# Moving each store of a log-softmax kernel into the middle of the next tile's exponentials

## Chip, cores, metric

One core of one Trainium2 chip. The time is that of one execution on the device, in microseconds (us). Every run told here was fast, with a granted clock of 1.0. A ratio between two kernels is the mean time of one kernel's fast runs over that of the other's fast runs of the same rounds, so it is not quite the ratio of the medians that are quoted beside it.

## The reference

```python
# x: float32, 16 x 512 x 50000
max_x = np.max(x, axis=-1, keepdims=True)
shifted = x - max_x
log_sum_exp = np.log(np.sum(np.exp(shifted), axis=-1, keepdims=True))
return (shifted - log_sum_exp).astype(np.float32)
```

1638.4 MB come in and as many go out.

## The kernel before

A tile is 32 rows of x, each cut over 4 partitions: 128 partitions of 12,500 numbers, 6.4 MB. There are 256 tiles and four buffers of that size. A buffer goes round like this: SP issues the load; VectorE (DVE) takes the maxima in four quarters; ScalarE (ACT) takes the four exponentials with their sums; the sums are joined; DVE subtracts in place; ACT issues the store; and SP, when that store has landed, issues the load of the tile four further on into the same buffer. The first and the last tile go in four parts.

```python
NBUF = 4
NS = 4
...
# SP: a load follows the store that frees its buffer
with sync.Fori(0, rounds - 1) as q:
    for i in range(NBUF):
        j = (i + 1) % NBUF
        take(sync, stored[j])
        load(j, src(q, i))
...
# DVE, one whole tile
take(vector, landed[j])
for c in range(NS):
    vector.tensor_reduce(out=negms[j][:, c : c + 1], in_=bufs[j][:, cols(c)],
                         op=ALU.max, axis=AX, negate=True).then_inc(...)
...
subtract(j, bufs[j])
...
# ACT, one whole tile
def store(j, dst, buf):
    subtracted.next(scalar.dma_start(out=dst, in_=buf)).then_inc(stored[j], 16)

def whole(j, dst):
    for c in range(NS):
        shifted.next(scalar.activation(out=dump, in_=bufs[j][:, cols(c)], func=ACT.Exp, ...)).then_inc(on_act.sem)
        on_act.next(scalar.nop())
    agreed.next(scalar.activation(out=scales[j], in_=negms[j], func=ACT.Exp, ...)).then_inc(rescaled.sem)
    log(j)
    store(j, dst, bufs[j])        # waits for DVE's subtraction of this tile
```

## Time and profile before

| | before |
|---|---|
| time, median of the first 3 runs | 7574.89 us (7571.26 to 7595.91) |
| span of its profile | 7612.1 us |
| busiest compute engine | DVE, 72% |
| DMA queues, share of 16 engines | 50.2% + 49.8% |

The costliest groups and the DMA issues of the page of before. A group's columns are count, busy time and mean ns of one, then the engine's idle time ahead of them and what ended most of it; an issue's are count, size and median us from issue to landing.

```profile
L274 ACT ACTIVATE dump<-buf,negm 128x3125 f32<-128x3125 f32 x1016 | 2914.3, 2868 | 3807.2 <-DVE negm L221 3710.5
L221 DVE TENSOR_REDUCE negm<-buf 128x1 f32<-128x3125 f32 x1016 | 3391.7, 3401 | 943.6 <-DVEq L47 943.6
...
buf<-in_x_dram SPq DMA_DIRECT2D x254, 6250.0 KB, 39.9
out_dram<-buf ACTq DMA_DIRECT2D x254, 6250.0 KB, 52.6
```

ACT's idle time is ended by DVE's maxima, and DVE's by landed loads.

### The profile page before, as it was taken

The numbers are of one execution on the slowest core, as the hardware profiler recorded it, in microseconds if no ns is written. First come the engines' busy times: TensorE is split into PE (matmuls) and PEld (weight loads), VectorE is DVE, ScalarE is ACT, GpSimd is POOL, SyncE is SP. The second block draws the span as 40 slices with busy tenths as digits, with TensorE's granted clock in tenths as the row PEclk, the third lists the DMA queues.
The fourth block names the chain that finished last, engine by engine and source line by source line (L and its number), as shares of the span: only waits on it lengthen the run. The fifth ranks groups of instructions, "written<-read, shape, count | busy, mean of one in ns | idle before, by whom it ended". The sixth has DMA issues, their size and how long they took to land. (4 is left out here: it accounts for less than half of the span.)

```text
span 7612.1 us, 14101 instructions
## 1 busy us (share of the span) xinstructions
PE 478.8 (6%) x2048; PEld 456.4 (6%) x2048; DVE 5445.7 (72%) x2842; ACT 3185.1 (42%) x2565; POOL 2.3 (0%) x10
## 2 busy tenths in 40 slices
PE   0000000000000000000000000000000000000000
PEld 0000000000000000000000000000000000000000
DVE  7777777777776777777767777777777777777777
ACT  4344444434444344443443444434434444344443
POOL 0000000000000000000000000000000000000000
DMA  9999999999999999999999999999999999999999
GB/s 423 434 433 433 434 434 434 433 433 434 434 433 432 432 432 431 431 432 428 429 429 429 426 427 429 431 430 432 432 431 431 433 433 433 434 433 431 432 433 393
DMA packets 75458, 3276.85 MB, mean 430 GB/s; under 512 B 8384, under 2 KB 8384, under 8 KB 8384
## 3 DMA queue, kind: packets, MB, share of 16 engines
q1 hardware_dynamic: 37728, 1638.42, 50.2%
q10 hardware_dynamic: 37728, 1638.42, 49.8%
q14 instruction: 2, 0.02, 0.0%
HBM read 1638.40 MB, written 1638.40 MB: 430 GB/s over the span
## 5 line engine op out<-in xcount | busy, mean ns | idle before, releaser
L274 ACT ACTIVATE dump<-buf,negm 128x3125 f32<-128x3125 f32 x1016 | 2914.3, 2868 | 3807.2 <-DVE negm L221 3710.5
L221 DVE TENSOR_REDUCE negm<-buf 128x1 f32<-128x3125 f32 x1016 | 3391.7, 3401 | 943.6 <-DVEq L47 943.6
L211 DVE TENSOR_SCALAR buf<-buf,negmax,logsum 128x12500 f32<-128x12500 f32 (+1 forms) x262 | 1739.7, 6640 | 553.9 <-ACT logsum L265 553.9
L324 PE MATMUL sums<-scaled,ones 128*128 128x1 f32 x2032 | 474.1, 355 | 7061.9 <-DVE scaled L232 7061.9
L324 PEld LDWEIGHTS sums<-scaled,ones 128*128 128x128 f32 x2032 | 452.4, 328 | 7083.6 <-DVE scaled L232 7083.6
L232 DVE TENSOR_TENSOR scaled<-scale,part 128x4 f32<-128x4 f32 x254 | 41.2, 162 | 575.4 <-ACT scale L282 575.4
L265 ACT ACTIVATE logsum<-sums 128x1 f32<-128x1 f32 x262 | 44.8, 171 | 552.3 <-PE sums L324 546.9
L274 ACT ACTIVATION_READ_ACCUMULATOR dump<-buf,negm 128x1 f32 x1016 | 189.4, 186 | 0.0
L282 ACT ACTIVATE scale<-negm,negmax 128x4 f32<-128x4 f32 x254 | 75.5, 297 | 23.5
L226 DVE TENSOR_REDUCE negp<-negm 128x1 f32<-128x4 f32 x254 | 39.9, 157 | 38.9 <-DVE negm L221 38.9
L206 DVE STREAM_TRANSPOSE negmax<-spread 128x32 f32<-128x32 f32 x262 | 55.5, 212 | 9.1
L190 DVE STREAM_TRANSPOSE allneg<-negp 128x32 f32<-128x32 f32 x262 | 55.4, 212 | 9.1
L193 DVE TENSOR_REDUCE rowneg<-allneg 128x8 f32<-128x32 f32 (+1 forms) x262 | 48.8, 186 | 9.1
L200 DVE COPY spread<-rowneg 128x32 f32<-128x32 f32 x262 | 47.5, 181 | 9.1
L293 ACT ACTIVATE dump<-buf,negmax 128x3125 f32<-128x3125 f32 x8 | 22.9, 2869 | 30.9 <-DVE negmax L206 30.9
L239 DVE TENSOR_REDUCE negp<-buf 128x1 f32<-128x3125 f32 x8 | 27.2, 3399 | 8.1 <-DVEq L47 8.1
L335 PE MATMUL sums<-sub_sum,ones 128*128 128x1 f32 x16 | 4.7, 363 | 59.0 <-ACT dump L293 59.0
L335 PEld LDWEIGHTS sums<-sub_sum,ones 128*128 128x128 f32 x16 | 4.0, 312 | 59.6 <-ACT dump L293 59.6
L308 ACT ACT_TABLE_LOAD x1 | 1.3, 1283 | 1.0 <-SPq L115 1.0
L293 ACT ACTIVATION_READ_ACCUMULATOR dump<-buf,negmax 128x1 f32 x8 | 1.5, 186 | 0.0
L144 POOL TENSOR_SCALAR_AFFINE_SELECT ones<-ones 128x128 f32<-128x128 f32 x2 | 0.9, 442 | 0.1
L148 POOL TENSOR_SCALAR_AFFINE_SELECT ones<-ones 128x128 f32<-128x128 f32 x2 | 0.9, 428 | 0.1
(5 smaller groups left out, 0.8 us busy)
## 6 DMA issues: line engine op xcount, KB each, us to landing
buf<-in_x_dram SPq DMA_DIRECT2D x254, 6250.0 KB, 39.9
out_dram<-buf ACTq DMA_DIRECT2D x254, 6250.0 KB, 52.6
buf<-in_x_dram SPq DMA_DIRECT2D x8, 1562.5 KB, 27.6
out_dram<-buf ACTq DMA_DIRECT2D x8, 1562.5 KB, 18.3
```

The source lines that it names most:

```text
L190: vector.transpose(out=allneg, in_=negp.to_broadcast([P, SQ]))
L193: vector.tensor_reduce(out=rowneg[:, : SQ // g], in_=allneg.rearrange("p (r g) -> p r g", g=g), op=op, axis=AX, negate=negate,)
L200: vector.tensor_copy(out=spread.rearrange("p (r g) -> p r g", g=g), in_=rowneg[:, : SQ // g, None].to_broadcast([P, SQ // g, g]),)
L206: vector.transpose(out=negmaxs[k], in_=spread)
L211: vector.tensor_scalar(out=buf, in0=buf, scalar1=negmaxs[k][:, 0:1], scalar2=logs[k], op0=ALU.add, op1=ALU.subtract,)
L221: vector.tensor_reduce(out=negms[j][:, c : c + 1], in_=bufs[j][:, cols(c)], op=ALU.max, axis=AX, negate=True,).then_inc(shifted.sem if c < ...
L226: vector.tensor_reduce(out=negp, in_=negms[j], op=ALU.min, axis=AX).then_inc(on_dve.sem)
L232: vector.tensor_mul(out=scaleds[j], in0=scales[j], in1=parts[j])
L265: scalar.activation(out=logs[k], in_=rowsums[k], func=ACT.Ln)
L274: scalar.activation(out=dump, in_=bufs[j][:, cols(c)], func=ACT.Exp, bias=negms[j][:, c : c + 1], scale=1.0, accum_out=parts[j][:, c : c + 1],
L282: scalar.activation(out=scales[j], in_=negms[j], func=ACT.Exp, bias=negmaxs[j][:, 0:1], scale=-1.0,)
L324: ins = tensor.matmul(rowsums[j], ones[G], scaleds[j][:, c : c + 1], start=c == 0, stop=c == NS - 1,)
```

## The change

Its intent is to keep ACT from standing still behind the subtraction and to issue the store of a tile two exponentials into the next one. In the loop's first lap there is no earlier tile, so the first whole tile is taken out ahead of it; after the last tile one store is left over.

```diff
+GATE = 2
...
-        def whole(j, dst):
+        def whole(j, dst=None):
             for c in range(NS):
+                if c == GATE and dst is not None:
+                    store((j - 1) % NBUF, dst, bufs[(j - 1) % NBUF])
                 shifted.next(
...
             log(j)
-            store(j, dst, bufs[j])
...
+        whole(1)
+        settle()
         dst = run(ot, 1, rounds)
         with scalar.Fori(0, rounds) as q:
             for i in range(NBUF):
-                whole((i + 1) % NBUF, dst(q, i))
+                whole((i + 2) % NBUF, dst(q, i))
             settle()
-        for t in tail:
-            whole(t % NBUF, ot[t])
+        for t in tail[1:]:
+            whole(t % NBUF, ot[t - 1])
+        store(t % NBUF, ot[t], bufs[t % NBUF])
```

## The prediction

> **What bounds the kernel now.** I read the page from the top: first the spans, then the row of slices, then the queues, then the waits, then the timeline of two tiles, and last the time from issue to landing of loads and stores in several windows. The page of the kernel before:
>
> ```profile
> span 7612.1 us, 14101 instructions
> ...
> PE 478.8 (6%) x2048; PEld 456.4 (6%) x2048; DVE 5445.7 (72%) x2842; ACT 3185.1 (42%) x2565; POOL 2.3 (0%) x10
> ...
> DMA  9999999999999999999999999999999999999999
> ...
> q1 hardware_dynamic: 37728, 1638.42, 50.2%
> q10 hardware_dynamic: 37728, 1638.42, 49.8%
> ...
> HBM read 1638.40 MB, written 1638.40 MB: 430 GB/s over the span
> ```
>
> No compute engine is busy for more than 72%, while the DMA row is 9 in every slice, and the two queues (one of loads, one of stores) take 50.2% + 49.8% = 100% of what 16 engines have in the span. The kernel moves the input in once and the output out once, and nothing else: the bytes are the bound. In the packet records of the trace a row of 50,000 bytes takes 1847 ns (the median at 150 to 600 us and again at 7000 to 7500 us). A tile is 128 rows in and 128 rows out over 16 engines, so 16 packets for each engine: 16 x 1.847 = 29.55 us. 256 tiles make 256 x 29.55 = 7565 us. The time before is 7574.89. Some 10 us, 0.13%, is all that lies over this floor, and it lies at the two ends.
>
> The waits say the same from the engines' side:
>
> ```profile
> DVE negm L221 <- DVEq L47: 943.6, 252, 4.8
> SPq L47 <- SPq L47: 7449.2, 256, 73.9
> ```
>
> VectorE stands 943.6 us for loads to land, 3.7 us in each tile, and the loading queue spends nearly the whole run waiting for stores to land, since a load takes the buffer of the store four tiles earlier. So DVE and ACT have room, and each waits for the DMA engines.
>
> One tile in the steady part (timeline: start, length, engine, line, operation):
>
> ```profile
> 3039.25 6.79 DVE L211 TENSOR_SCALAR buf<-buf,negmax,logsum 128x12500 f32<-128x12500 f32 x1 [2.17 <-ACT logsum L265]
> 3046.07 0.34 ACTq L269 DMA_DIRECT2D out_dram<-buf  x1
> 3049.64 13.35 DVE L221 TENSOR_REDUCE negm<-buf 128x1 f32<-128x3125 f32 x4 [3.60 <-DVEq L47]
> 3053.09 2.87 ACT L274 ACTIVATE dump<-buf,negm 128x3125 f32<-128x3125 f32 x1 [13.87 <-DVE negm L221]
> ...
> 3056.40 2.87 ACT L274 ACTIVATE dump<-buf,negm 128x3125 f32<-128x3125 f32 x1 [0.32 <-DVE negm L221]
> ...
> 3059.72 2.87 ACT L274 ACTIVATE dump<-buf,negm 128x3125 f32<-128x3125 f32 x1 [0.32 <-DVE negm L221]
> ```
>
> The store goes at 3046.07, as soon as the subtraction ends. The third exponential of the next tile starts at 3059.72; the change puts the store just ahead of it. **The delay of each store is therefore about 3059.4 - 3046.1 = 13.3 us.** The question is whether the store that is delayed had anything to do in those 13.3 us. The answer is in the landings (the view of the store's line at 150 to 450 us, then at 7000 to 7500):
>
> ```profile
> DMA to landing us min/median/max: 52.6/52.6/52.7
> ```
> ```profile
> DMA to landing us min/median/max: 42.6/43.0/44.4
> ```
>
> Stores come every 29.6 us and take 52.6 us to land, so when one is issued the one ahead of it still has 52.6 - 29.6 = 23.0 us to go: the new one only stands in the ring. Late in the run that backlog is 43.0 - 29.6 = 13.4 us. For loads the same views give 39.0 us (backlog 9.4) early and 49.2 us (19.6) late.
>
> **What the Trainium skill says.** "DMA: Bandwidth & Descriptors", section Specifications, gives a fabric ceiling of 435 GB/s; the page's best slices show 434 and the packets 16 x 50,000 bytes / 1.847 us = 433 GB/s, so the trace agrees that nothing is left to gain in rate. The same page, section "Queues, rings and completion order", says that each engine takes turns, packet by packet, between the queue rows that have work; the 50.2% and 49.8%, and loads and stores both landing every 29.6 us, agree. It also says that the engines of one transfer finish independently. The landing records show how far: one store's first and last engine land 2.6 us apart at 200 us of the run and 25 us apart at 7480 us. "Perfetto Trace Analysis", section "Summary: the profiler window per engine type", says that the window of such a DMA instruction leaves out the movement of data: here the store's instruction shows 0.34 us against 43 to 55 us to landing, so the landings, not the instruction, must be read.
>
> **The change part by part.**
> It removes nothing and adds no work: 262 stores before and after, of the same sizes, the same arithmetic, the same loads.
>
> *The store's place on ACT.* Before, ACT stood still behind the subtraction (6.79 us) to issue the store. Then it stood another 7 us in any case, as the next exponentials need the next maxima, which DVE makes only after the subtraction. Freeing ACT there is worth 0. In the new place the issue costs ACT 0.34 us and two register operations (0.037 + 0.029 us), 0.4 us in all, ahead of the third exponential, where ACT had 0.32 us of idle time. The third exponential may start 0.1 us later; the fourth has 0.38 us of idle time ahead of it and takes that up. DVE is not touched. Sum on the path: 0.
>
> *The 13.3 us delay.* On the engine that lands last, backlog of the store ring at issue becomes 23.0 - 13.3 = 9.7 us early, and 13.4 - 13.3 = 0.1 us late. In neither does that ring run dry before its next store arrives, or barely, so each store lands when it did, the load behind it is issued when it was, and the period stays 29.55 to 29.6 us. And should the store ring be empty for a while, the load ring has 9 to 20 us of its own, and the engine works on loads at full speed meanwhile: no byte is lost. Engines that run ahead of the last one (up to 25 us late in the run) may idle a little; they are not the ones that set a landing.
>
> *Slack of the loop.* A buffer's cycle is 4 x 29.6 = 118.4 us. Alone on the engines a load takes 8 x 1.847 = 14.8 us and a store as much. From a load's landing to its store is now 13.35 + about 6 + 6.79, 26.4 us, and will be 26.4 + 3.6 + 9.7 = about 39.7 us. 14.8 + 39.7 + 14.8 = 69.3 us against 118.4: four buffers carry the delay with 49 us to spare.
>
> *The start.* Tile 1's store moves from 63.9 to about 73.6 us. The stores of the first tile's parts fill the ring until 79 us, so nothing is lost.
>
> *The end.* The last but one whole tile's store moves from 7546 to about 7559 us; the last one goes at once, as before (7575.5). In the slices of 5 us the DMA share falls to 0.18 and 0.13 at 7565 to 7575 us: after the last load all waits for tile 254's arithmetic, then the last tile's four parts. That chain hangs on the load that lands at 7549.4 us, which the change does not make later. The hole of about 11 us only moves ahead of the delayed store. Worth 0, give or take 3 us.
>
> *Less room between engines.* With 13.3 us less queued, an engine that stalls can be less far behind before the others wait for it. In the trace the gaps between engines build up over the whole run and not tile by tile, so I take 0 to 10 us, 3 as the middle: a guess. Sum: 7574.9 + 0 + 0 + 3 = 7578 us.
>
> **The rivals.**
> *A new wait (slower).* If stores had nothing queued before them, a later store would mean a later landing, a later load and a later tile. The wait of 13.3 us is real for the engines that land first (late in the run the first engine lands 18 us after issue, ahead of the next issue). Against it: they have 25 us of lead. If it did hold on every engine it could still not pass the loop's 69 us. The worst I can make of it is a period lost in pure-load and pure-store phases: at the start a load part of 1.6 MB alone takes 3.75 us, 427 GB/s against 433, 1.4% slower. If all of the run became such phases: 7575 x 1.014 = 7680 us.
> *A gain (faster).* Loads get the engines to themselves for a while after each subtraction, and ACT is free of a wait. For it: DVE waits 3.7 us per tile for loads. Against it: the byte floor of 7565 us. Even with both ends hidden the gain is 0.1%; over 2% would need 29.0 us per tile, 442 GB/s, which no slice shows.
> *ACT becomes late.* 0.4 us in each tile on the path would be 254 x 0.1 = 25 us at most if nothing took it up; DVE's wait of 3.7 us does.
>
> **Range and chances.** 7578 us; the floor of 7565 puts the low end at 7562 (runs of before went down to 7571), and 7604 leaves room for the spread of before (up to 7596) and some lost lead. Faster by over 2% is all but excluded by the bytes, slower by over 2% needs rival one in a form that the backlog speaks against.
>
> **What would show it.** The DMA row still all 9 and both queues near 50%; the period of stores still 29.6 us; time to landing of stores shorter by about 13 us (about 39 early) while that of loads stays near 39 early; DVE's wait for loads still about 940 us; the third exponential's idle time ending at the store's issue. Wrong I would be if the slices fell below 9, or if loads' landings stretched and DVE's wait with them.

## The result and the profile after

| | before | after |
|---|---|---|
| median of 6 runs | 7577.02 us | 7573.78 us |
| lowest to highest | 7571.26 to 7610.34 | 7570.39 to 7591.33 |
| ratio of fast runs, 95% interval | | 0.9993 (0.997 to 1.0015) |
| span of the profile | 7612.1 us | 7569.8 us |

The time is the same. The two profiles differ by 42 us, though, which is the first thing to be explained. The page after (its span, its row of slices, its queues and DMA issues) and its wait of DVE for loads:

```profile
span 7569.8 us, 13853 instructions
...
DMA  9999999999999999999999999999999999999999
...
q1 hardware_dynamic: 37728, 1638.42, 50.1%
q10 hardware_dynamic: 37728, 1638.42, 50.0%
...
HBM read 1638.40 MB, written 1638.40 MB: 433 GB/s over the span
...
buf<-in_x_dram SPq DMA_DIRECT2D x254, 6250.0 KB, 39.9
out_dram<-buf ACTq DMA_DIRECT2D x254, 6250.0 KB, 38.3
```
```profile
DVE negm L223 <- DVEq L49: 890.1, 251, 4.0
```

The queues are as full as they were. Loads take as long to land as before (39.9 us), stores 14.3 us less (38.3 after 52.6). The timeline of one tile after shows where the store stands now:

```profile
2998.84 6.79 DVE L213 TENSOR_SCALAR buf<-buf,negmax,logsum 128x12500 f32<-128x12500 f32 x1 [2.17 <-ACT logsum L267]
3009.18 13.35 DVE L223 TENSOR_REDUCE negm<-buf 128x1 f32<-128x3125 f32 x4 [3.55 <-DVEq L49]
...
3019.11 0.34 ACTq L271 DMA_DIRECT2D out_dram<-buf  x1
3019.50 2.87 ACT L279 ACTIVATE dump<-buf,negm 128x3125 f32<-128x3125 f32 x1 [0.57 <-DVE negm L223]
...
3022.62 2.87 ACT L279 ACTIVATE dump<-buf,negm 128x3125 f32<-128x3125 f32 x1
```

The subtraction ends at 3005.63 and the store goes at 3019.11, 13.5 us later. The third exponential has 0.57 us of idle time ahead of it where it had 0.32, and the fourth has none where it had 0.38: the cost of the issue is taken up within the tile.

**The 42 us between the profiles.** The packet records tell where they are. A packet is the transfer of one partition's 50,000 bytes; the whole tiles have 65,024 of them. Their median is 1847 ns in both profiles, but the sum of what is over 1847 ns, divided by 16 engines, is 37.3 us before and 4.6 us after. So 33 of the 42 us are stretched packets. The first experiment asks whether they belong to the kernel.

### The profile page after: what moved, and what is told of

Same layout as the page of the kernel before. It is cut to its first block, busy times and chain, and to the rows that moved or that the text cites. A ratio compares the mean times of both kernels' runs of the same rounds, so it can differ in the third digit from the quotient of the medians.

```text
span 7569.8 us, 13853 instructions
## 1 busy us (share of the span) xinstructions
PE 478.9 (6%) x2048; PEld 456.5 (6%) x2048; DVE 5445.6 (72%) x2842; ACT 3185.1 (42%) x2565; POOL 2.3 (0%) x10
## 6 DMA issues: line engine op xcount, KB each, us to landing
buf<-in_x_dram SPq DMA_DIRECT2D x254, 6250.0 KB, 39.9
out_dram<-buf ACTq DMA_DIRECT2D x254, 6250.0 KB, 38.3
out_dram<-buf ACTq DMA_DIRECT2D x8, 1562.5 KB, 22.2
```

## The experiments

The profiles of the same kernels are compared by packets as above; "excess" is the sum of all time over 1847 ns in such packets, over 16 engines. The first four ran on one chip, the next four on another, the next three on a third, and the last by itself; each group had its own runs of before beside it, and its ratios are to those. A run is named by the delay that was planned with a store every 29.6 us. Where the period grew, the delay grew with it: the medians that were measured over 150 tiles are 13.5 us in after, 17.9 for "16.7", 20.3 for "20", 30.5 for "30", 51.8 for "43" and 116.3 for "72".

**1. The kernel before, again** (no edit).

> The kernel before, unchanged, run against itself. The profile of before that the study began with (span 7612.1 us) and the one of after (7569.8) differ by 42 us although the timed medians are equal. Theory O (packets are stretched from outside in some executions): packets of 50,000 bytes that take over 1.9 us were 2062 in that profile of before and 232 in that of after, with 597 and 73 us of excess over 1847 ns; over 16 engines that is 37 and 5 us, most of the 42. If it comes from outside, this profile may well be quiet: span near 7570, excess under 150 us. Theory K (it belongs to the kernel before, whose stores start at another moment): the excess is again near 600 us and the span near 7610. Times: ratio 1.000 within 0.3% under both.

Measured: 7571.07 us (7570.92 to 7597.09) beside 7587.97 us of the same kernel in the same rounds, ratio 0.998 (0.9957 to 1.0003). Its page and wait:

```profile
span 7569.2 us, 14101 instructions
...
HBM read 1638.40 MB, written 1638.40 MB: 433 GB/s over the span
```
```profile
DVE negm L221 <- DVEq L47: 889.1, 252, 3.7
```

The excess is 2.4 us. The 42 us do not belong to the kernel before: a quiet execution of it is 0.6 us shorter than the profiled one of after, with the same wait of DVE. What stretches packets in some of the executions is not shown; runs of before went from 7571 to 7619 us. For the comparison with after this profile is to be used and not the first.

**2. The delay undone.** The change's own loop with the store ahead of the first exponential, where it goes at once when its subtraction is done.

```diff
-GATE = 2
+GATE = 0
```

> The change with its store put ahead of the first exponential of the next tile and not of the third: the loop is restructured as in the change, but the store is issued when its subtraction is done, as before; the delay of 13.3 us is undone. Theory A (bytes bound the kernel, the delay only shortens the time a store stands in its ring): 7575 us, ratio to before 1.000 within 0.3%; time from issue to landing of stores back at about 52 us. Rival (the delay gives something and the restructuring costs as much, or the reverse): off 1.000 by over 0.5%.

Measured: 7575.68 us (7570.71 to 7595.77), ratio 0.9988 (0.9959 to 1.0016), span 7569.0. Time to landing of stores, then of loads, at 1000 to 2000 us of this kernel, and the same two of after:

```profile
DMA to landing us min/median/max: 52.4/52.5/52.7
DMA to landing us min/median/max: 39.0/39.2/39.3
```
```profile
DMA to landing us min/median/max: 38.8/39.1/39.3
DMA to landing us min/median/max: 38.9/39.2/39.4
```

With the same loop, undoing the delay gives stores their 52.5 us back, 13.4 us more than after's 39.1, and leaves loads at 39.2 us and the time where it was. That is the prediction's mechanism: the delay only shortens a store's stand in its ring. The restructuring costs nothing and hides nothing.

**3 and 4. A delay of 43 us and of 72 us.** The store of tile t goes two, then three tiles later, at the same place among the exponentials.

```diff
-    store((j - 1) % NBUF, dst, bufs[(j - 1) % NBUF])
+    store((j - LAG) % NBUF, dst, bufs[(j - LAG) % NBUF])   # LAG = 2, then 3
```

> Each store waits one tile more: it goes ahead of the third exponential of the tile after the next, 43 us after its subtraction. Theory A, in the form of a loop: tile t+4 can start its maxima no sooner than its store was issued plus a store and a load alone on the engines, 10.1 + 29.6 us and some 3 us for two landings, after tile t+2 started; that is 2 periods of 21.4 us at least, under the byte floor of 29.55. So 7575 us, within 0.5%. Rival B (the limit is the backlog that stands in the rings, 33 us of stores and loads together in the trace of before): 43 us exceed it by 10, the loop of four buffers becomes 59.2 + 69.3 = 128.5 us, 32.1 us in each tile, 8220 us (8.5% slower).

> Each store waits two tiles more (ahead of the third exponential of the third tile after, 72 us after its subtraction). Theory A: now one period alone must hold 10.1 us of maxima and exponentials, a store and a load alone (29.6 us) and about 3 us for two landings: 42.7 to 43.5 us in each tile, 10,900 to 11,100 us in all, with the DMA share near 0.69. Rival B: 59.2 + 98.6 = 157.8 us in four buffers, 39.5 us each, 10,100 us. Rival D (where a store is issued does not matter as long as all bytes flow): 7575 us.

Measured: 8690.91 us at 43 us, ratio 1.1446 (1.1414 to 1.1477), and 11,258.19 us at 72 us, ratio 1.483 (1.4779 to 1.488). The windows of 1000 to 4000 us of the two (columns: window, length, busy time and count of PE, PEld, DVE, ACT, POOL, clock, DMA share, GB/s):

```profile
1000.00:4000.00 3000.00, 164.34 (x704) 156.79 (x704) 1881.20 (x977) 1104.27 (x887) 0.00 (x0) 1.00 0.92 377
```
```profile
1000.00:4000.00 3000.00, 126.91 (x544) 121.08 (x544) 1446.64 (x749) 845.57 (x680) 0.00 (x0) 1.00 0.69 290
```

At 72 us the chain is bare: 9.9 us from the start of a tile's maxima to the store, then 16.2 us to its landing and 17.6 us to the load's (medians of 3000 to 3600 us), 43.7 us, against 43.9 to 44.5 us from one tile to the next in the timeline. The first theory had it right but for 1 us of landing time; the share of 0.69 is as told beforehand. At 43 us both theories fell: no loss was expected by the first, 8.5% by the second, 14.5% came. The DMA engines are idle for 8% of the time, tiles come in turn 27 and 41 us apart, and the excess is 452 us, over a third of the loss and all of it in packets of loads. So the loop bound of the prediction says when loss is certain; it doesn't say that there is none below.

**5 and 6. A delay of 20 us and of 30 us.** The store goes behind the fourth exponential; then, for 30 us, it waits for the subtraction of the next tile as well.

```diff
# 5: after the loop over c
+            if dst is not None:
+                store((j - LAG) % NBUF, dst, bufs[(j - LAG) % NBUF])   # LAG = 1
# 6: LAG = 2, GATE = 0, and the wait one subtraction later
+            ins.wait_op(subtracted.sem, subtracted.seen + later, "sem-ge")   # later = 1
```

> The store goes behind the fourth exponential of the next tile: 20.0 us after its subtraction instead of 13.3. Backlog theory: the store ring of the kernel before holds 23.0 us at a store's issue, and both rings together 33, so nothing is lost: 7575 us, within 0.5% of before, stores landing 32 to 33 us after issue. A theory that the change stands at the edge of what the loop carries would have it 1% slower or more.

> The store waits for the subtraction of the next tile too: 29.6 us after its own. The store ring's backlog of 23.0 us is passed, the 33 us of both rings are not: 3.6 us are left. Backlog theory with both rings counted: the loop is 59.2 + 26.4 + 29.6 = 115.2 us for 4 tiles of 29.55 (118.2), so still 7575 to 7650 us. With the store ring alone counted: 6.6 us too much for a store, up to 254 x 6.6 / 4 = 420 us, 8000 us.

Measured: 7723.39 us (7676.63 to 7783.08) at 20 us, ratio 1.0183 (1.0112 to 1.0255); 7938.95 us at 30 us, ratio 1.0455 (1.0414 to 1.0496). At 20 us the backlog theory, which expected no loss, fell; the rival, 1% or more at the edge of what the loop carries, came true. At 30 us the sum of both rings (7575 to 7650 us) fell; the sum of the store ring alone gave up to 8000, and 7939 lies near it, but not for its reason, which is waiting: the excess there is 273 us of the 368 that the span is over that of after. The page at 20 us:

```profile
q10 hardware_dynamic: 37728, 1638.42, 50.4%
q1 hardware_dynamic: 37728, 1638.42, 49.6%
...
HBM read 1638.40 MB, written 1638.40 MB: 424 GB/s over the span
```

The engines are as busy as ever (100.0%) and move 424 GB/s, not 433. No wait shows the loss; the packets do. The excess is 150.7 us, and the span is 151.5 us over that of after: the whole loss is stretched packets. Of the excess, 59% is in stores' packets that begin within 3 us of a store's issue, 6% of all packets. Between 200 and 7000 us of the run a load and a store are in flight at every moment (looked at each 0.1 us) if each counts until its last engine has landed it. By its first engine's landing there is no load in flight for 12% of the time and no store for 14%: some engines have one empty ring for a while in each period.

**7 and 8. Two buffers, without and with the change.**

```diff
-NBUF = 4
+NBUF = 2
```

> The kernel before with two buffers instead of four. One buffer computes (26.4 us from landing to store) while the other is stored and loaded (29.6 us alone, some 4 us for two landings): (26.4 + 33.6) / 2 = 30.0 us in each tile where the two just fit, 7700 us; sharing of the engines between one buffer's load and the other's store may bring it up to 33 us, 8450 us. Backlog theory (every load and store at half rate): (59.2 + 26.4) / 2 = 42.8 us, 10,930 us.

> The change with two buffers instead of four. A tile's maxima can start only when the store issued in the middle of the tile before and the load behind it have both landed: 10.1 + 34.0 us, as the run with a delay of 72 us showed (44.1 us in each tile with one buffer to spare, 11,258 us). So 11,250 us again, 30% or more over the two-buffer kernel before: the same edit that costs nothing with four buffers. A theory that the edit is harmless by itself expects it equal to the two-buffer kernel before.

Measured: 8631.1 us without and 11,280.0 us with the change, each over the same runs of before 1.1415 and 1.4864; the one over the other 1.30. The same edit that costs nothing with four buffers costs 30% with two, and the time is that of the 72 us delay with four (11,258), as the shared chain of store, load and 9.9 us demands. The two-buffer kernel without the change was expected at 7700 to 8450 us and lies above that, far under the 10,930 us of the backlog theory; its excess is 407 us.

**9. A delay of 16.7 us.**

```diff
-GATE = 2
+GATE = 3
```

> The store goes ahead of the fourth exponential of the next tile: 16.7 us after its subtraction, between the change (13.3, no loss) and the run with 20.0 us (150 us lost, all of it in packets longer than 1847 ns, most of them stores that start within 2 us of their issue). Dry-ring theory (time is lost as soon as a store finds its ring empty on some of the engines): in the quiet profile with the delay undone stores land 52 us after issue on the last engine and some 3 us sooner on the first, so 52 - 3 - 16.7 = 32 us are left at 29.55 us per tile, no engine's ring runs dry, and the time is 7575 us, under 0.4% from before. Graded theory (the loss grows evenly beyond 13.3 us): half of the 150 us, 7650 us, 1% slower.

Measured: 7823.34 us (7780.66 to 7867.93), ratio 1.0315 (1.0283 to 1.0347). Both theories fell: it is slower than the 20 us delay (on another chip, but the intervals of the two ratios lie apart). Windows of this run:

```profile
200.00:600.00 400.00, 24.27 (x104) 23.16 (x104) 287.56 (x147) 168.81 (x135) 0.00 (x0) 1.00 1.00 433
600.00:1000.00 400.00, 26.14 (x112) 24.94 (x112) 281.54 (x151) 166.95 (x136) 0.00 (x0) 1.00 1.00 433
1000.00:2000.00 1000.00, 59.75 (x256) 57.00 (x256) 696.74 (x357) 405.61 (x325) 0.00 (x0) 1.00 1.00 419
2000.00:4000.00 2000.00, 121.34 (x520) 115.77 (x520) 1383.18 (x716) 809.61 (x652) 0.00 (x0) 1.00 1.00 416
```

The DMA share stays at 1.00, while the rate is 433 GB/s for the first 1000 us, the rate of after, and 416 to 419 later. The kernel runs free of loss until something sets in. The landing records of the engines show what differs between the two stages (medians, us from the end of the issuing instruction, 0.3 us after its start, to landing on the engine that lands first and on the one that lands last):

```
delay      window, us    loads first/last   stores first/last
13.5       200-600       35.9 / 38.1        36.1 / 39.6
(after)    4000-4500     36.2 / 39.7        34.6 / 37.9
16.7       200-600       32.7 / 35.1        35.9 / 39.4
           4000-4500     21.5 / 37.7        20.6 / 39.9
20.0       200-600       33.8 / 36.5        32.1 / 34.7
           4000-4500     26.1 / 36.9        24.7 / 35.8
```

In after, the 16 engines stay within 5 us of each other. With 16.7 and 20 us they start as close and drift 11 to 19 us apart. It is one engine that falls behind: at 16.7 us and 4000 to 4500 us of the run, 15 engines land a store 20.6 to 23.3 us after issue and the last at 39.9. The 15 are done well ahead of the next issue, so that their ring is empty when the next store comes. The excess at 16.7 us is 224 us of a loss in span of 254.

Are the drift and the empty rings the cause of the loss? Two looks at the records say that they are not enough. First, the profile of before that the study began with, which has no delay, drifts further. At 7000 to 7400 us its loads land 18.9 us after issue on the first engine and 48.8 on the last, its stores 19.4 and 42.6, and 13 of the 16 engines have landed both within 23 us, with a period of 29.6. There too both rings of the 13 run empty in every period, and yet the rate is that of after:

```profile
7000.00:7400.00 400.00, 26.13 (x112) 24.93 (x112) 283.25 (x145) 163.76 (x134) 0.00 (x0) 1.00 1.00 433
```

The excess of before in that stage is 0.07 us in a tile, against 1.0 us at 4000 to 4500 us of the run with 16.7. Second, the engine that falls behind sets the period, and its own rings never run empty: with 16.7 us its loads take 37.7 us to land and its stores 39.9, with an issue every 30.8. Its packets can be followed, each from the end of the one before, in 60 of 97 periods between 4000 and 7000 us: 16 in a period, 29.51 us without stretching (as in after), with an excess of 1.02 us on the mean, most of it in its loads. So its packets are stretched although its rings are full. Nor does the margin at the start tell the two cases apart: early, the first engine had 3.2 us left over a period of 29.5 (loads, at 16.7) or 2.6 us (stores, at 20), and after never falls below 4.3 us (stores, at 6500 to 7000 us), but before, which drifted, started with 6.1 us (loads). What makes the loss at 16.7 and 20 us is not shown.

**10, 11 and 12. Stores in two halves.** Each store is cut into two of 6,250 columns. In 10 both go at once when the subtraction is done; in 11 the second half goes 20 us later, behind the fourth exponential; in 12 both go there.

```diff
+        def store_half(j, dst, h):
+            ins = scalar.dma_start(out=half(dst, h), in_=half(bufs[j], h))
+            if h == 0:
+                subtracted.next(ins)
+            ins.then_inc(stored[j], 16)
...
-            take(sync, stored[j])
+            take(sync, stored[j], 32)
```

> Control of the next run: each store is cut into two of 6,250 columns, both issued when the subtraction is done. Packets of 25,000 bytes instead of 50,000, the same bytes. Both theories: 7575 us, within 0.5% of before.

> The first half of each store is issued when the subtraction is done, the second half 20.0 us later, behind the fourth exponential of the next tile, the very place that cost 1.8% for whole stores. Dry-ring theory: the first half (14.8 us at half rate) and the store ahead keep the ring filled over the 20 us, so nothing is lost: equal to the control, within 0.5%. Rival (the place is what costs: a store's issue between the fourth exponential and the scale delays ACT and with it DVE, or a store started late in a tile runs into the loads): 1 to 2% slower than the control.

> Both halves of each store are issued 20.0 us after the subtraction, behind the fourth exponential of the next tile: the delay of the run that lost 1.8% with whole stores, with packets of 25,000 bytes. In the control and in the run with the second half late, loads landed 25 to 27 us after issue (the engines take turns by packet, and a load's packets are twice as long), so the load ring ran dry in every tile and all of the slack stood in the store ring; both ran at 7621 us. Theory S (a loss comes when the store ring runs dry): 118.2 - 27 - 46.4 = 45 us for a store, 15 us more than its 29.5, no loss: 7621 us, within 0.5% of the control. Theory T (the slack of the loop as a whole is too small at a delay of 20 us, wherever it stands): again 1 to 2% over the control, 7700 to 7770 us.

Measured: 7622.27 us in 10, 7620.36 us in 11, 7628.48 us in 12; over before 1.0049 (1.0032 to 1.0066), 1.0045 (1.0028 to 1.0062) and 1.0057 (1.0038 to 1.0075). The cut itself costs 0.5%. The place of the store costs nothing: the same 20 us at the same place, which lost 1.8% with whole stores, lose 0.1% here (12 over 10, which ran on two chips; each over its own runs of before, 0.6% and 0.5%). Loads of 12 at 1000 to 2000 us:

```profile
DMA to landing us min/median/max: 26.2/27.4/28.6
```

They land 27 us after issue and not 37 as in the uncut kernel with this delay. "DMA: Bandwidth & Descriptors" of the Trainium skill, section "Queues, rings and completion order", has the engines take turns by packet; a load's packet is still 50,000 bytes and a store's is 25,000, so loads get two thirds of an engine while both have work, and this run agrees with it: a load's 8 packets in turn with 8 of a store would take 8 x (1.847 + 0.928) = 22.2 us (an estimate from the medians of its packets), and the first engine lands a load 25.4 us after issue, where equal shares would take 8 x 2 x 1.847 = 29.6 us. All of the slack moves to the stores. Theory T (the slack of the loop as a whole decides) falls, at least with stores' packets of 25,000 bytes. Theory S (a store ring that runs dry) is not contradicted by run 12, but the two looks under 9 speak against it as the whole cause, and the shorter packets could themselves be what keeps the engines together; no run tells these apart. That a load ring runs dry in every tile costs little here: the excess of loads in 10 is 39.5 us.

## Why the prediction was right, and where its working was not

- *Bytes bound the kernel* at 7565 us: right. Quiet profiles of before, of the undone delay and of after span 7569.2, 7569.0 and 7569.8 us. The 4 to 5 us that are left over the floor were not split between the two ends and the stretched packets, which come to 2.3 to 4.6 us in these profiles. The prediction read a page whose span was 37 us over the 7574.89 us that it explained, and did not ask why.
- *The store is 13.3 us late and only stands less long in its ring*: right; 13.5 us, and stores land in 39.1 us where they took 52.5, with loads at 39.2 us in both (experiment 2).
- *ACT takes up the 0.4 us of the issue*: right, with 0.25 us on the third exponential instead of 0.1, none of it left after the fourth.
- *Late in the run only 0.1 us of backlog is left, and stores land in about 30 us*: wrong. The late figures, 43.0 us for stores and 49.2 for loads, came from a profile with stretched packets. In a quiet one stores still take 51.3 us at 7000 to 7400 us and loads 40.4, and in after 37.9 and 40.4.
- *The end*: the hole of 11 us ahead of the last stores was also a trait of that one execution. In after a hole stands at 7555 to 7560 us, behind the last loads, and in the quiet run of before at 7550 to 7560. The stores of the last two whole tiles go at 7505.9 and 7522.0 us, and not at 7559 and 7575.5. Worth nothing, as said.
- *"Four buffers carry the delay with 49 us to spare"* and *"no byte is lost"* while the other ring has work: wrong, though the forecast did not hang on them. With 3.4 us more of planned delay the time is 3.15% longer, though the engine that lands last has a load and a store in flight throughout. What failed is the step from the loop's sum to "no loss": it counts how long engines have work, and not how fast a packet goes. The excess over packets of 1847 ns was 4.6 us in the change and 151 to 452 us in runs 3 to 9. The sum was right only where it says that loss is certain (runs 4 and 8).
- *Less room between engines, 3 us as a guess*: the quiet profiles of before and after are 0.6 us apart. The danger that was named showed at the next 3.4 us of delay: the engines drift and 254 us are lost. That the drift is what costs them is not shown (run 9). That the change lies on the near side of this edge is luck as far as the prediction goes: its sums would have passed 16.7 and 20 us as well.
- *Slips that cost nothing*: the rival "ACT becomes late" names 0.4 us in each tile and multiplies 254 by 0.1; 254 x 0.4 would be 102 us. The shares of 50.2% and 49.8% follow from equal bytes and do not test whether engines take turns by packet; run 12 does. And that the engines of a transfer finish independently stands on the same page of the Trainium skill, but in the section "Why a DMA increments its semaphore by 16 and not by 1".

What stays open: what drives the engines apart; why a delay of 16.7 us costs more than one of 20; and what stretches a packet. In runs 5 and 9 the stretch gathers where transfers start: the packets that begin within 2 us of a store's issue or 9 us of a load's are 37% and 35% of all and hold 72% and 87% of the excess. In the first profile of before they hold 19% with 33% of the packets, so this is no rule, and no run took a cause away by itself. No version beat both kernels, and with 4 us over the byte floor none was to be looked for.

## What to carry to other kernels

In this kernel, which the DMA engines bound, moving a store's issue by 13.5 us was free: every engine still had the store before it in its ring. The same held at the start of the run with 16.7 us, and 254 us were lost later in that run. So compare time to landing, on the first engine too, with the period before moving an issue, and measure with a few us more delay to see how near the edge is. A sum that says "enough buffers" is a bound for certain loss and not a promise. And a busy DMA row is not a rate: look at GB/s and at the length of packets, and take a second profile before explaining half a per cent.

## What the Trainium skill lacked or had wrong

- "Perfetto Trace Analysis", section "Identifying the Most-Contended Engine", says that DMA should be judged by bytes moved and not by occupancy, since 16 engines make occupancy misleading. The runs agree and give another reason: one and the same kernel shows a share of 1.00 at 433 GB/s and at 416 (run 9), because a stretched packet counts as busy.
- "DMA: Bandwidth & Descriptors", section "Specifications", gives a first-byte latency of about 0.6 us for the sync and scalar queues. Run 4, where loads and stores start on idle engines, agrees: a load's first packet begins 0.6 us after the end of the issuing instruction, a store's 0.5 us. The page does not say that this first packet can itself take longer: there, the first one of a load on each engine takes 2607 ns on the mean and the others 1848; the first of a store 1884 and the others 1852. Nor does it say when packets amid a stream stretch, as in runs 5 and 9.
- No page says how far the 16 engines drift apart within one stream of transfers: 3 us between the first and the last to land, growing to 19 us in run 9 with a loss of 3%, and to 30 us in the first profile of before, whose span is 0.6% over that of the quiet one.
